# One-hots of four tokens from one VectorE comparison, with the gate's two parts multiplied in by GpSimd and ScalarE

## The chip, the cores and the metric

One NeuronCore of a Trainium2 chip runs the whole program. The metric is the device time of one launch in microseconds (us), less is better. In this text PE is TensorE (PEld its weight loads), DVE is VectorE, ACT is ScalarE, POOL is GpSimd, SP the engine that issues most DMAs.

## The reference

A two-layer encoder on 256 tokens of width 1024. Each layer has an attention part and then PEER, a retrieval of experts, and the change is in PEER alone. For each token, 8 heads choose 16 of 16384 experts each; an expert is a pair (i1, i2) of key numbers under 128:

```python
best, pos = lax.top_k(cand, PEER_TOPK)
expert = jnp.take_along_axis(cand_idx, pos, axis=-1)      # i1 * 128 + i2
gate = jax.nn.softmax(best, axis=-1)
...
u = w_down[e_blk]
a = jnp.einsum('td,ted->te', x_blk, u).astype(jnp.float32)
hg = (jax.nn.gelu(a, approximate=False) * g_blk).astype(w_up.dtype)
return jnp.einsum('te,ted->td', hg, w_up[e_blk]).astype(x_blk.dtype)
```

The output is the float32 result of both layers.

## The kernel before, in words

The kernel gathers no expert. It computes every expert for every token and multiplies by a gate that is zero for those not chosen. `peer(li)` runs twice, once for each layer, in this order:

1. Queries and key scores.
2. The loop over `b0` (lines 1017 to 1039): 128 blocks of 128 experts, two a round. A block is 24 matmuls of 128x256 (`d`, in `proj`): weights and x are each split into a high and a low fp32r part, and three of the four products are summed. ScalarE then takes the GELU of a round's two blocks into `A`, a view of the arena [128, block, token].
3. The up projection (`rows`, tile `y`), 128 blocks again.

Beside the first 50 or so blocks of the loop the generator `choose` finds the 128 (head, k) pairs of every token, mostly on VectorE. It ends with the gates and indices transposed, a pair on each partition and a token in each column (tile `gT`), and the lines 973 to 984: `gt` is the gate times 2^14, `g16`/`gh` its half-precision part, `gr` the rest as a share of that part, `i1t` and `i2t` the two key numbers.

From then on each round also **places** gates. `prepare(g4)` (lines 989 to 998) makes, for a group of four tokens, three half-precision matrices per token, [128 pairs, 128 keys]: V, the one-hot of i2; U, the one-hot of i1 times the gate; L, U times `gr`. V is made on GpSimd, U on VectorE (one instruction, comparison and product), L on ScalarE. `place(g4, done)` (lines 1000 to 1012) multiplies them on TensorE: for each token V is the stationary operand, U and L are moved through it and summed in a tile `G`, whose element [i2, i1] is the token's gate for that expert. `G` is multiplied into the blocks of `A` that have had their GELU already (L1011, VectorE, reading G and A) and copied into the columns of `A` of the blocks to come (L1009, ScalarE), where the later GELU is multiplied in (L1029 on ScalarE, L1030 on VectorE).

The loop places two groups in a round and then prepares the next two. `VU` and `U` come from the pool `ohp`, which has two buffers of each, so a group's one-hots can be made only after TensorE has read those of the group two before it, and they have to be there when TensorE comes to the G matmuls one round later. The weight stream `ws` works three blocks ahead in four buffers: a cast to `hi` on ScalarE (L97), `lo` = raw - hi on VectorE (L101). The order of instructions on each engine is found by a scheduler at build time, except where a chain fixes it. Each engine then works its queue in that order.

Of the kernel before, what the change touches and what calls it, by code (L numbers as in the profile page):

```python
# [10 lines left out]
F32 = mybir.dt.float32  # L11
F32R = mybir.dt.float32r
F16 = mybir.dt.float16
U32 = mybir.dt.uint32
AF = mybir.ActivationFunctionType
ALU = mybir.AluOpType
AX = mybir.AxisListType

P = 128
T = 256  # L20
# [5 lines left out]
NKEYS = 128  # L26
# [18 lines left out]
WARM = 9  # L45
EARLY = 11264
GSCALE = 2.0 ** 14
TINY = 2.0 ** -40
DSA_POOL = 3
MAGIC = 12582912.0  # L50

# [111 lines left out]
def tile_trunk(ctx: ExitStack, tc: tile.TileContext, ins, out: bass.AP):  # L163
    nc = tc.nc
    def pool(name, bufs, **kw):
        return ctx.enter_context(tc.tile_pool(name=name, bufs=bufs, **kw))

    const = pool("const", 1)
# [3 lines left out]
    ohp = pool("ohp", 2)  # L172
# [9 lines left out]
    def ps(name):  # L182
        return psp.tile([P, 512], F32, tag="ps", name=name)

    def py(i, name):
        return pyp.tile([P, 512], F32, tag=f"py{i}", name=name)
# [5 lines left out]
    keep = [dram.tile([P, D], F32, tag=f"x{t}", name=f"x{t}") for t in range(2)]  # L192
    xh = const.tile([P, NC, T], F32R, tag="xh", name="xh")
    xl = const.tile([P, NC, T], F32R, tag="xl", name="xl")
    i1t = const.tile([P, T], F32, tag="i1t", name="i1t")
    i2t = const.tile([P, T], F32, tag="i2t", name="i2t")
    gt = const.tile([P, T], F32, tag="gt", name="gt")
    gr = const.tile([P, T], F32, tag="gr", name="gr")
    iota16 = const.tile([P, P], F16, tag="iota16", name="iota16")
    iotac = const.tile([P, CELLS, TOPK], F16, tag="iotac", name="iotac")  # L200
    arena = big.tile([P, 32768], F32, tag="arena", name="arena")
# [39 lines left out]
    def pe(emit):  # L241
        return link("pe", emit)
# [4 lines left out]
    def mm(o, l, r, start, stop):  # L247
        return pe(lambda: nc.tensor.matmul(o, l, r, start=start, stop=stop, skip_group_check=True))  # L248
# [606 lines left out]
    def peer(li):  # L855
# [14 lines left out]
        hot = ar.ring(2, TOPK, CELLS)  # L870
# [4 lines left out]
        tail = s[0].rearrange("p a b -> p (a b)")  # L875
# [46 lines left out]
        def choose():  # L922
            for t in range(2):
# [21 lines left out]
                for h in range(HEADS + 1):  # L945
                    if h < HEADS:
                        o, same = hot(), eq[h % 2]
                        nc.vector.tensor_tensor(same, iotac, pos16[t][:, h, None, :].to_broadcast([P, CELLS, TOPK]),  # L948
                                                op=ALU.is_equal)
# [20 lines left out]
                nc.tensor.transpose(pg[:, tsl], best[t].rearrange("p h k -> p (h k)"), ident)  # L970
                nc.tensor.transpose(pg[:, T + t * P : T + (t + 1) * P], exp_[t].rearrange("p h k -> p (h k)"), ident)
            e = pg[:, T:]
            g16, gh, gl = tail[:, 0 : T // 2].bitcast(F16), tail[:, T : 2 * T], tail[:, 2 * T : 3 * T]
            nc.vector.tensor_scalar(gt, pg[:, :T], GSCALE, None, op0=ALU.mult)
            nc.vector.tensor_copy(g16, gt)
            nc.vector.tensor_copy(gh, g16)
            nc.vector.tensor_tensor(gl, gt, gh, op=ALU.subtract)
            nc.vector.tensor_scalar(gh, gh, TINY, None, op0=ALU.max)
            nc.vector.reciprocal(gr, gh)
            nc.vector.tensor_tensor(gr, gr, gl, op=ALU.mult)  # L980
            nc.vector.tensor_scalar(i1t, e, 1.0 / NKEYS, -(NKEYS - 1) / (2.0 * NKEYS), op0=ALU.mult, op1=ALU.add)
            nc.vector.tensor_scalar(i1t, i1t, MAGIC, None, op0=ALU.add)
            nc.vector.tensor_scalar(i1t, i1t, -MAGIC, None, op0=ALU.add)
            nc.vector.scalar_tensor_tensor(i2t, i1t, -float(NKEYS), e, op0=ALU.mult, op1=ALU.add)  # L984
            yield

        onehot = {}

        def prepare(g4):
            hot16 = ohp.tile([P, 2, 4, P], F16, tag="V", name="VU")  # L990
            low16 = ohp.tile([P, 4, P], F16, tag="U", name="U")
            onehot[g4] = []
            for t in range(4 * g4, 4 * g4 + 4):
                V, U, L = hot16[:, 0, t % 4, :], hot16[:, 1, t % 4, :], low16[:, t % 4, :]
                nc.gpsimd.tensor_scalar(V, iota16, i2t[:, t : t + 1], None, op0=ALU.is_equal)  # L995
                nc.vector.tensor_scalar(U, iota16, i1t[:, t : t + 1], gt[:, t : t + 1], op0=ALU.is_equal, op1=ALU.mult)  # L996
                nc.scalar.mul(L, U, gr[:, t : t + 1])  # L997
                onehot[g4].append((V, U, L))

        def place(g4, done):  # L1000

            p = py(g4 % 4, f"G{g4}")
            for j, (V, U, L) in enumerate(onehot.pop(g4)):
                mm(p[:, j * P : (j + 1) * P], V, U, True, False)
                mm(p[:, j * P : (j + 1) * P], V, L, False, True)
            pv = p.rearrange("p (t b) -> p b t", b=P)
            tsl = slice(4 * g4, 4 * g4 + 4)
            if done < P:
                nc.scalar.mul(A[:, done:, tsl], pv[:, done:, :], 1.0 / GSCALE)  # L1009
            if done:  # L1010
                nc.vector.scalar_tensor_tensor(A[:, :done, tsl], pv[:, :done, :], 1.0 / GSCALE, A[:, :done, tsl],  # L1011
                                               op0=ALU.mult, op1=ALU.mult)

        bg = choose()
        groups = prepared = 0
        ready = False
        for b0 in range(0, NKEYS, 2):
            p = ps(f"d{b0}")
            pv = p.rearrange("p (j t) -> p j t", t=T)
            for j in range(2):  # L1020
                proj(pv[:, j, :], ws.get())
                for _ in range(STEPS[(b0 + j) % len(STEPS)]):
                    if not ready and next(bg, StopIteration) is StopIteration:
                        ready = True
            t0 = 4 * groups
            if t0 < T:
                nc.scalar.activation(A[:, b0 : b0 + 2, t0:], pv[:, :, t0:], AF.Gelu)
            if t0 > 0:
                nc.scalar.activation(pv[:, :, :t0], pv[:, :, :t0], AF.Gelu)  # L1029
                nc.vector.tensor_tensor(A[:, b0 : b0 + 2, :t0], A[:, b0 : b0 + 2, :t0], pv[:, :, :t0], op=ALU.mult)  # L1030
            while groups < prepared:
                place(groups, b0 + 2)
                groups += 1
            if ready:
                left = max(1, (NKEYS - 8 - b0) // 2)
                want = min(64 - groups, -(-(64 - groups) // left))
                for _ in range(want):
                    prepare(prepared)
                    prepared += 1
# [170 lines left out]
```

## Time and profile before

| what | value |
|---|---|
| median of 3 runs | 1865.2 us (1864.09 to 1866.58) |
| the profiled execution's own time | 1863.45 us |
| its span, first to last instruction | 1861.6 us |
| granted TensorE clock, mean | 0.998 of full speed |
| busy: PE / DVE / ACT / POOL | 1838.8 / 1326.6 / 1050.9 / 565.4 us |
| first G matmul of layer 0, of layer 1 | at 312.9 us, at 1259.2 us |
| last G matmul | at 1478.4 us |

Busy time is the sum over the span of time in which an engine had an instruction of the program at work. A matmul's record is longer than the step from one to the next, since they are pipelined: a d matmul's record lasts 0.28 us, and 48 of them take 5.71 us. So TensorE's pace is read from the starts. Waits are named by what ended them.

### The profile page before, as it was taken

Reading aid. Unit: us, or ns where it says so; the run is one execution under the profiler, and the core shown is the slowest. Engines: PE = TensorE matmul, PEld = TensorE weight load, DVE = VectorE, ACT = ScalarE, POOL = GpSimd, SP = SyncE. Lnnn points to the kernel's source line nnn. Section 1 sums busy time; section 2 is a strip of 40 time slices with the busy share of each in tenths; the row PEclk is TensorE's granted clock in tenths of the full one; section 3 lists DMA queues with packets and bytes.
Section 4 is the critical chain, followed back from the end, with each engine's and each line's share of the span. In section 5 each row is a group of like instructions: output and inputs, shape, how many; then the busy total and the mean of one; then the engine's idle time right before and its main releaser. Section 6 shows DMA issues by size and latency. Waiting matters only on the chain. (4 is left out here: it accounts for less than half of the span.)

```text
span 1861.6 us, 33296 instructions
## 1 busy us (share of the span) xinstructions
PE 1838.8 (99%) x12495; PEld 1653.3 (89%) x12495; DVE 1326.6 (71%) x2738; ACT 1050.9 (56%) x1826; POOL 565.4 (30%) x646
## 2 busy tenths in 40 slices
PE   9999999999999999999999999999999999999998
PEld 8899999999998888888888899999999988888886
DVE  6689986788865555555687789957888765555555
ACT  6655456777764444444466445548777654444443
POOL 2002443999930000000021004519999600000000
PEclk9999999999999999999999999999999999999999
DMA  6554655444456555556646455554444575555553
GB/s 236 192 175 166 192 194 180 150 154 154 158 194 213 189 186 191 186 187 191 205 154 227 153 169 181 175 196 153 159 151 157 169 229 190 186 189 191 184 190 114
DMA packets 93474, 335.52 MB, mean 180 GB/s; under 512 B 10368, under 2 KB 11392, under 8 KB 93312
## 3 DMA queue, kind: packets, MB, share of 16 engines
q1 hardware_dynamic: 93024, 332.87, 54.4%
q8 instruction: 98, 1.61, 0.4%
q14 instruction: 64, 0.52, 0.1%
q10 hardware_dynamic: 288, 0.52, 0.1%
HBM read 329.16 MB, written 4.19 MB: 179 GB/s over the span
## 5 line engine op out<-in xcount | busy, mean ns | idle before, releaser
L101 DVE TENSOR_TENSOR lo<-raw,hi 128x1024 fp32r<-128x1024 f32 (+1 forms) x581 | 715.7, 1234 | 341.9 <-ACT hi L97 341.2
L97 ACT CAST hi<-raw 128x1024 fp32r<-128x1024 f32 (+1 forms) x583 | 609.8, 1047 | 580.1 <-PE d L248 255.3
L248 PE MATMUL d<-xh,hi 128*128 128x256 f32 x2048 | 579.4, 283 | 0.0
L248 PE MATMUL d<-xh,lo 128*128 128x256 f32 x2048 | 573.0, 280 | 0.6 <-DVE lo L101 0.6
L248 PE MATMUL d<-xl,hi 128*128 128x256 f32 x2048 | 573.3, 280 | 0.0
L995 POOL TENSOR_SCALAR VU<-iota,i2t 128x128 f16<-128x128 f16 x512 | 430.0, 858 | 110.8 <-DVE i2t L984 98.8
L248 PEld LDWEIGHTS d<-xh,lo 128*128 128x128 f32 x2048 | 384.7, 188 | 1.0 <-DVE lo L101 1.0
L248 PEld LDWEIGHTS d<-xh,hi 128*128 128x128 f32 x2048 | 385.1, 188 | 0.0
L248 PEld LDWEIGHTS d<-xl,hi 128*128 128x128 f32 x2048 | 384.6, 188 | 0.0
L248 PE MATMUL y<-hi,xh 128*128 128x512 f32 x1088 | 344.3, 395 | 0.1
L248 PE MATMUL y<-lo,xh 128*128 128x512 f32 x1088 | 344.2, 395 | 0.0
L248 PE MATMUL y<-hi,xl 128*128 128x512 f32 x1088 | 343.8, 394 | 0.0
L339 POOL TENSOR_TENSOR st<-st,mhalf 128x1 f32<-128x1 f32 x8 | 4.4, 554 | 853.3 <-DVE st L337 853.3
L248 PEld LDWEIGHTS y<-lo,xh 128*128 128x128 f32 x1088 | 203.7, 187 | 50.1 <-DVE lo L101 0.3
L248 PEld LDWEIGHTS y<-hi,xl 128*128 128x128 f32 x1088 | 203.7, 187 | 50.0
L248 PEld LDWEIGHTS y<-hi,xh 128*128 128x128 f32 x1088 | 203.3, 187 | 50.1 <-DVE xl L276 0.5
L996 DVE TENSOR_SCALAR VU<-iota,i1t,gt 128x128 f16<-128x128 f16 x512 | 139.5, 350 | 57.8 <-PE G L248 31.5
L997 ACT ACTIVATE U<-VU,gr 128x128 f16<-128x128 f16 x512 | 170.1, 399 | 0.8 <-DVE gr L980 0.7
L1051 ACT CAST xh<-arena 128x512 fp32r<-128x512 f32 x128 | 79.4, 621 | 154.5 <-PE y L248 149.2
L1052 DVE TENSOR_TENSOR xl<-arena,xh 128x512 fp32r<-128x512 f32 x128 | 88.3, 693 | 82.2 <-ACT xh L1051 82.2
L950 POOL TENSOR_TENSOR arena<-arena 128x800 f32<-128x800 f16 x32 | 78.9, 2486 | 40.8 <-DVE arena L948 39.9
L248 PE MATMUL G<-VU 128*128 128x128 f16 x512 | 71.5, 222 | 6.3 <-DVE VU L996 3.7
(225 smaller groups left out, 1805.3 us busy)
## 6 DMA issues: line engine op xcount, KB each, us to landing
raw<-in_down SPq DMA_DIRECT2D x256, 512.0 KB, 3.3
raw<-in_up SPq DMA_DIRECT2D x256, 512.0 KB, 4.3
raw<-in_peer_q SPq DMA_DIRECT2D x24, 512.0 KB, 4.1
raw<-in_dsa_qk SPq DMA_DIRECT2D x16, 512.0 KB, 3.3
raw<-in_mla_w_o SPq DMA_DIRECT2D x8, 512.0 KB, 7.3
arena<-in_peer_q SPq DMA_DIRECT2D x8, 512.0 KB, 4.2
raw<-in_dsa_v SPq DMA_DIRECT2D x8, 512.0 KB, 4.4
raw<-in_dsa_w_o SPq DMA_DIRECT2D x8, 512.0 KB, 3.9
```

Of the source, the lines that this page charges most:

```text
L97: nc.scalar.copy(hi, raw)
L101: self.dve(lambda: nc.vector.tensor_tensor(lo, raw, hi.bitcast(F32), op=ALU.subtract))
L248: return pe(lambda: nc.tensor.matmul(o, l, r, start=start, stop=stop, skip_group_check=True))
L339: nc.gpsimd.tensor_tensor(st[:, 5:6], st[:, 4:5], mhalf, op=ALU.pow)
L950: nc.gpsimd.tensor_tensor(o.rearrange("p k c -> p c k"), same, cell[t][:, h, :, None].to_broadcast([P, CELLS, TOPK]), op=ALU.mult)
L995: nc.gpsimd.tensor_scalar(V, iota16, i2t[:, t : t + 1], None, op0=ALU.is_equal)
L996: nc.vector.tensor_scalar(U, iota16, i1t[:, t : t + 1], gt[:, t : t + 1], op0=ALU.is_equal, op1=ALU.mult)
L997: nc.scalar.mul(L, U, gr[:, t : t + 1])
L1051: nc.scalar.copy(hh, a)
L1052: nc.vector.tensor_tensor(al, a, hh.bitcast(F32), op=ALU.subtract)
```

## The change

- `prepare` makes both one-hots of four tokens, of i2 and of i1, with one VectorE comparison of 128x1024 elements (tile `hot`). Both its inputs and its output are 16-bit: `iota16` is repeated over the eight one-hots, and each token's index over 128 elements. The indices are kept as half-precision numbers in `place16`.
- The gate no longer enters in the comparison. GpSimd multiplies the four one-hots of i1 by the half-precision gates (one product of 128x512, tile `gate`, part 0). ScalarE multiplies the same one-hots by the rest, `rest` = gt - gate16, token by token (part 1).
- `place` makes the same matmuls: `hot[:, 0]` stationary, the two parts of `gate` moved.
- The lines after the transposes get shorter: no clamp, no reciprocal, no product with it.

```diff
@@ -45,7 +45,6 @@
 WARM = 9
 EARLY = 11264
 GSCALE = 2.0 ** 14
-TINY = 2.0 ** -40
 DSA_POOL = 3
 MAGIC = 12582912.0
 
@@ -192,10 +191,9 @@
     keep = [dram.tile([P, D], F32, tag=f"x{t}", name=f"x{t}") for t in range(2)]
     xh = const.tile([P, NC, T], F32R, tag="xh", name="xh")
     xl = const.tile([P, NC, T], F32R, tag="xl", name="xl")
-    i1t = const.tile([P, T], F32, tag="i1t", name="i1t")
-    i2t = const.tile([P, T], F32, tag="i2t", name="i2t")
-    gt = const.tile([P, T], F32, tag="gt", name="gt")
-    gr = const.tile([P, T], F32, tag="gr", name="gr")
+    place16 = const.tile([P, 2, T], F16, tag="place16", name="place16")
+    gate16 = const.tile([P, T], F16, tag="gate16", name="gate16")
+    rest = const.tile([P, T], F32, tag="rest", name="rest")
     iota16 = const.tile([P, P], F16, tag="iota16", name="iota16")
     iotac = const.tile([P, CELLS, TOPK], F16, tag="iotac", name="iotac")
     arena = big.tile([P, 32768], F32, tag="arena", name="arena")
@@ -970,39 +968,38 @@
                 nc.tensor.transpose(pg[:, tsl], best[t].rearrange("p h k -> p (h k)"), ident)
                 nc.tensor.transpose(pg[:, T + t * P : T + (t + 1) * P], exp_[t].rearrange("p h k -> p (h k)"), ident)
             e = pg[:, T:]
-            g16, gh, gl = tail[:, 0 : T // 2].bitcast(F16), tail[:, T : 2 * T], tail[:, 2 * T : 3 * T]
+            gt, i1 = tail[:, 0:T], tail[:, T : 2 * T]
             nc.vector.tensor_scalar(gt, pg[:, :T], GSCALE, None, op0=ALU.mult)
-            nc.vector.tensor_copy(g16, gt)
-            nc.vector.tensor_copy(gh, g16)
-            nc.vector.tensor_tensor(gl, gt, gh, op=ALU.subtract)
-            nc.vector.tensor_scalar(gh, gh, TINY, None, op0=ALU.max)
-            nc.vector.reciprocal(gr, gh)
-            nc.vector.tensor_tensor(gr, gr, gl, op=ALU.mult)
-            nc.vector.tensor_scalar(i1t, e, 1.0 / NKEYS, -(NKEYS - 1) / (2.0 * NKEYS), op0=ALU.mult, op1=ALU.add)
-            nc.vector.tensor_scalar(i1t, i1t, MAGIC, None, op0=ALU.add)
-            nc.vector.tensor_scalar(i1t, i1t, -MAGIC, None, op0=ALU.add)
-            nc.vector.scalar_tensor_tensor(i2t, i1t, -float(NKEYS), e, op0=ALU.mult, op1=ALU.add)
+            nc.vector.tensor_copy(gate16, gt)
+            nc.vector.tensor_tensor(rest, gt, gate16, op=ALU.subtract)
+            nc.vector.tensor_scalar(i1, e, 1.0 / NKEYS, -(NKEYS - 1) / (2.0 * NKEYS), op0=ALU.mult, op1=ALU.add)
+            nc.vector.tensor_scalar(i1, i1, MAGIC, None, op0=ALU.add)
+            nc.vector.tensor_scalar(i1, i1, -MAGIC, None, op0=ALU.add)
+            nc.vector.tensor_copy(place16[:, 1, :], i1)
+            nc.vector.scalar_tensor_tensor(place16[:, 0, :], i1, -float(NKEYS), e, op0=ALU.mult, op1=ALU.add)
             yield
 
         onehot = {}
 
         def prepare(g4):
-            hot16 = ohp.tile([P, 2, 4, P], F16, tag="V", name="VU")
-            low16 = ohp.tile([P, 4, P], F16, tag="U", name="U")
-            onehot[g4] = []
-            for t in range(4 * g4, 4 * g4 + 4):
-                V, U, L = hot16[:, 0, t % 4, :], hot16[:, 1, t % 4, :], low16[:, t % 4, :]
-                nc.gpsimd.tensor_scalar(V, iota16, i2t[:, t : t + 1], None, op0=ALU.is_equal)
-                nc.vector.tensor_scalar(U, iota16, i1t[:, t : t + 1], gt[:, t : t + 1], op0=ALU.is_equal, op1=ALU.mult)
-                nc.scalar.mul(L, U, gr[:, t : t + 1])
-                onehot[g4].append((V, U, L))
+            hot = ohp.tile([P, 2, 4, P], F16, tag="V", name="hot")
+            gate = ohp.tile([P, 2, 4, P], F16, tag="U", name="gate")
+            four = slice(4 * g4, 4 * g4 + 4)
+            nc.vector.tensor_tensor(hot, iota16[:, None, None, :].to_broadcast([P, 2, 4, P]),
+                                    place16[:, :, four, None].to_broadcast([P, 2, 4, P]), op=ALU.is_equal)
+            nc.gpsimd.tensor_tensor(gate[:, 0], hot[:, 1], gate16[:, four, None].to_broadcast([P, 4, P]), op=ALU.mult)
+            for j in range(4):
+                t = 4 * g4 + j
+                nc.scalar.mul(gate[:, 1, j, :], hot[:, 1, j, :], rest[:, t : t + 1])
+            onehot[g4] = hot, gate
 
         def place(g4, done):
 
             p = py(g4 % 4, f"G{g4}")
-            for j, (V, U, L) in enumerate(onehot.pop(g4)):
-                mm(p[:, j * P : (j + 1) * P], V, U, True, False)
-                mm(p[:, j * P : (j + 1) * P], V, L, False, True)
+            hot, gate = onehot.pop(g4)
+            for j in range(4):
+                for i in range(2):
+                    mm(p[:, j * P : (j + 1) * P], hot[:, 0, j, :], gate[:, i, j, :], i == 0, i == 1)
             pv = p.rearrange("p (t b) -> p b t", b=P)
             tsl = slice(4 * g4, 4 * g4 + 4)
             if done < P:
```

The build also puts instructions in another order. Line numbers of the changed kernel are one to three lower for the same statement.

VectorE, a placing round in the middle of layer 0, before. VU are the one-hots, lo the low weight parts, L1011 and L1030 the products with G and with d:

```order
L996 TENSOR_SCALAR VU<-iota_96,i1t,gt 128x128 x8
L101 TENSOR_TENSOR lo_6590<-raw_6395,hi_6589 128x1024
L1011 SCALAR_TENSOR_TENSOR arena<-G_6538,arena 128x106x4
L1011 SCALAR_TENSOR_TENSOR arena<-G_6549,arena 128x106x4
L1030 TENSOR_TENSOR arena<-arena,d_6474 128x2x192
L101 TENSOR_TENSOR lo_6620<-raw_6479,hi_6619 128x1024
L996 TENSOR_SCALAR VU<-iota_96,i1t,gt 128x128 x8
```

And now, in a placing round of the same layer:

```order
L988 TENSOR_TENSOR hot<-iota_95,place_92 128x1024 x2
L100 TENSOR_TENSOR lo_4846<-raw_4675,hi_4845 128x1024
L1008 SCALAR_TENSOR_TENSOR arena<-G_4806,arena 128x78x4
L1008 SCALAR_TENSOR_TENSOR arena<-G_4817,arena 128x78x4
L1027 TENSOR_TENSOR arena<-arena,d_4742 128x2x80
L100 TENSOR_TENSOR lo_4876<-raw_4747,hi_4875 128x1024
L988 TENSOR_TENSOR hot<-iota_95,place_92 128x1024 x2
```

Two comparisons of 1024 elements stand where eight of 128 stood; the rest of the round keeps its order.

TensorE, the first placing round of layer 0, before. G_3802 and G_3813 are the first two groups, d_3852 the block pair of that round:

```order
L248 LDWEIGHTS VU
L248 MATMUL G_3802<-U,VU 128x128
L248 LDWEIGHTS VU
L248 MATMUL G_3802<-VU 128x128
L248 MATMUL d_3852<-xh,hi_3681 128x256
L248 LDWEIGHTS VU
L248 MATMUL G_3802<-U,VU 128x128
L248 LDWEIGHTS VU
L248 MATMUL G_3802<-VU 128x128
L248 MATMUL d_3852<-xl,hi_3681 128x256
```

And now, the end of the same two groups and the d matmuls behind them:

```order
L246 LDWEIGHTS hot
L246 MATMUL G_3797<-gate,hot 128x128
L246 LDWEIGHTS hot
L246 MATMUL G_3797<-gate,hot 128x128
L246 MATMUL d_3824<-xh,hi_3677 128x256
L246 MATMUL d_3824<-xl,hi_3677 128x256
L246 MATMUL d_3824<-xh,lo_3678 128x256
L246 MATMUL d_3824<-xh,hi_3677 128x256
```

Before, the G matmuls of the first two rounds were scattered among those of d; now each round has its 16 in one piece, from the first on. From the third round on both kernels read 16 of G, 48 of d.

## Rows read from the trace of the kernel before

**Rows 1.** The page, part 1: busy us (share of the span) xinstructions.

```profile
PE 1838.8 (99%) x12495; PEld 1653.3 (89%) x12495; DVE 1326.6 (71%) x2738; ACT 1050.9 (56%) x1826; POOL 565.4 (30%) x646
```

**Rows 2.** The chain that ended last, in order of time: start, us, what.

```profile
1466.35 5.71 PE d L248 x48
1472.07 0.46 PE G L248 x8
```

**Rows 3.** Timeline of PE, first G matmuls of rounds: start, us, engine, line, operation.

```profile
312.91 0.23 PE L248 MATMUL G<-VU 128*128 128x128 f16 x1
...
335.38 0.23 PE L248 MATMUL G<-VU 128*128 128x128 f16 x1
342.00 0.23 PE L248 MATMUL G<-VU 128*128 128x128 f16 x1
...
525.19 0.23 PE L248 MATMUL G<-VU 128*128 128x128 f16 x1
1259.22 0.23 PE L248 MATMUL G<-VU 128*128 128x128 f16 x1
...
1281.70 0.23 PE L248 MATMUL G<-VU 128*128 128x128 f16 x1
...
1471.91 0.23 PE L248 MATMUL G<-VU 128*128 128x128 f16 x1
```

**Rows 4.** Waits: who waited for whom; us in total, times, longest.

```profile
PEld L248 <- POOL VU L995: 12.0, 33, 0.7
```

**Rows 5.** Groups by line, 335.38 to 525.19 us: count, busy us, mean ns, idle before.

```profile
L995 POOL TENSOR_SCALAR VU<-iota,i2t 128x128 f16<-128x128 f16 x225 | 189.4, 859 | 2.4 <-PE G L248 2.0
L997 ACT ACTIVATE U<-VU,gr 128x128 f16<-128x128 f16 x224 | 74.7, 399 | 0.0
```

**Rows 6.** Timelines of PE, DVE and POOL in one placing round.

```profile
403.18 0.23 PE L248 MATMUL G<-VU 128*128 128x128 f16 x1
403.89 2.06 DVE L996 TENSOR_SCALAR VU<-iota,i1t,gt 128x128 f16<-128x128 f16 x8 [0.69 <-PE G L248]
404.88 0.66 POOL L995 TENSOR_SCALAR VU<-iota,i2t 128x128 f16<-128x128 f16 x1
405.88 1.21 DVE L101 TENSOR_TENSOR lo<-raw,hi 128x1024 fp32r<-128x1024 f32 x1
406.12 1.44 POOL L995 TENSOR_SCALAR VU<-iota,i2t 128x128 f16<-128x128 f16 x1
407.01 0.91 DVE L1011 SCALAR_TENSOR_TENSOR arena<-G,arena 128x336 f32<-128x336 f32 x2
```

**Rows 7.** Timelines of POOL and DVE, in choose of layer 0 and in dsa.

```profile
255.03 1.72 POOL L950 TENSOR_TENSOR arena<-arena 128x800 f32<-128x800 f16 x1 [0.43 <-DVE arena L948]
255.71 1.98 DVE L101 TENSOR_TENSOR lo<-raw,hi 128x1024 fp32r<-128x1024 f32 x1
...
930.84 0.69 DVE L495 TENSOR_TENSOR arena<-qi,arena 128x512 f32<-128x512 f32 x1 [1.16 <-ACT arena L492]
930.89 1.30 POOL L496 TENSOR_TENSOR arena<-arena 128x512 f32<-128x512 f32 x1 [19.88 <-ACT arena L492]
```

**Rows 8.** Timelines of DVE and POOL, in dsa, 982.8 to 985.

```profile
982.86 1.21 DVE L101 TENSOR_TENSOR lo<-raw,hi 128x1024 fp32r<-128x1024 f32 x1
983.78 1.45 POOL L496 TENSOR_TENSOR arena<-arena 128x512 f32<-128x512 f32 x1 [3.84 <-ACT arena L492]
984.00 1.38 DVE L801 TENSOR_SCALAR arena<-arena 128x256 f32<-128x256 f32 x1
```

**Rows 9.** Two lines: count, ns min/median/max, first and last start, forms.

```profile
L948 DVE TENSOR_TENSOR arena<-iotac,arena x32: 552/590/1070, 179.4 to 1198.4; 128x800 f16<-128x800 f16 x32
L496 POOL TENSOR_TENSOR arena<-arena x13: 742/1297/1908, 28.2 to 1003.8; 128x512 f32<-128x512 f32 x12, 128x256 f32<-128x256 f32 x1
```

**Rows 10.** Two lines of the placing rounds, same columns.

```profile
L1011 DVE SCALAR_TENSOR_TENSOR arena<-G,arena x128: 386/513/659, 318.3 to 1480.4; 128x232 f32<-128x232 f32 x4, 128x240 f32<-128x240 f32 x4, 128x248 f32<-128x248 f32 x4, 128x256 f32<-128x256 f32 x4
L1030 DVE TENSOR_TENSOR arena<-arena,d x70: 157/438/684, 325.4 to 1498.0; 128x512 f32<-128x512 f32 x6, 128x16 f32<-128x16 f32 x2, 128x32 f32<-128x32 f32 x2, 128x48 f32<-128x48 f32 x2
```

## The prediction

> **What bounds the kernel now.** I read the page's head first: TensorE is busy for 1838.8 us, 99% of the span, so time can only be won where TensorE waits or runs in a worse order [rows 1]. The chain of waits then tells what a stretch without loss looks like: 48 products of d take 5.71 us, eight of G 0.46 us [rows 2]. The change touches only the placing stretch of the two peer layers, in which every round of two blocks runs 16 G products and 48 d products. I went through TensorE's timeline for the starts of G groups [rows 3]. A good round takes 342.00 - 335.38 = 6.62 us. The 28 rounds from 335.38 to 525.19 take 189.81 us where 28 x 6.62 = 185.36 would do: 4.45 us lost; in layer 1, 1281.70 to 1471.91 is 190.21: 4.85 us lost. Ahead of them stand three rounds' worth of products (144 of d, 48 of G) in 335.38 - 312.91 = 22.47 and 1281.70 - 1259.22 = 22.48 us, against 3 x 6.62 = 19.86: 2.61 and 2.62 us lost. Together **14.5 us** of the whole run.
>
> Who causes it: TensorE's weight loads wait on GpSimd's one-hots [rows 4], and GpSimd has almost no idle time in the 189.81 us: its 225 comparisons keep it busy for 189.4 us, 0.859 each, while ScalarE's 224 products take 74.7 us [rows 5]. Eight comparisons by 0.859 are 6.87 us a round, more than TensorE's 6.62. So GpSimd sets the round, not TensorE. A comparison alone takes 0.66 us; one that meets VectorE's subtraction lo of 405.88 takes 1.44 [rows 6]: GpSimd stands still while that runs.
>
> **The port.** This sharing decides what the new code costs. While a GpSimd product of two SBUF inputs runs from 255.03 to 256.75, lo of 255.71 takes 1.98 us, not 1.22: it starts at 256.47, 0.28 before GpSimd ends [rows 7]. A VectorE operation with one input in PSUM is untouched: L495 takes its 0.69 us beside a GpSimd product of 1.30 [rows 7]. So two-input work from SBUF runs on one of the two engines at a time. Who goes first: the GpSimd product of 983.78 finds lo at work until 984.07 and takes 1.45 us, 0.15 over its 1.30; VectorE's next operation, issued at 984.00, then takes 1.38 and so lets GpSimd through [rows 8]. The engine that waited goes first.
>
> **Part by part.**
> - *GpSimd*: 512 comparisons go, 128 products of 128x512 come. Bounds for one: 512/800 of the 1.72 us row, 1.10 [rows 7]; the median of 128x512 f32 products, 1.30 [rows 9]. I take 1.20, midway. Two a round are 2.4 us in place of 6.87.
> - *VectorE*: eight comparisons a round (2.06 us together [rows 6]) go, two of 1024 elements come. Bounds for one: L948 compares 800 16-bit pairs in 0.552 us when alone [rows 9], which is 0.7 us for 1024; lo has 1024 elements and takes 1.22 [rows 6]. I take 1.22: in the new operation one index stands still for 128 elements, which makes it unlike L948, whose two inputs both run on. [...]
> - *ScalarE*: still eight products a round, 74.7 / 224 = 0.33 us each [rows 5]. They now stand in one block ahead of a hi, not around it. The first four can start when the first comparison ends (1.92, below), the others when the second does (3.06), so the last ends at 4.4 to 4.7, two microseconds ahead of the next G. The hi behind them and its lo feed a block three ahead, so TensorE does not wait for it.
> - *TensorE*: same products, in groups of 16 from the first round. This and an unhindered GpSimd would return all 14.5 us.
> - *Index chain*: four operations less and one more, on 256 elements. The first G follows the transposes by 96 products of d, twice 5.71 us [rows 2], which cover it before and now; nothing lies on the path. DMAs and SP's queue are unchanged.
>
> **What is late next.** VectorE's order in a round is: comparison, comparison, lo, two products with G (L1011), one with d (L1030), lo. The first comparison starts 0.7 us after the first G product, when that buffer is read (403.18 and 403.89, [rows 6]); operations follow 0.08 us before the end of the one before, so those of 1.22 come every 1.14 us. The second comparison ends at 3.06. The first gate product, waiting, starts 0.14 before that, at 2.92, and lo waits until 0.28 before its end: 0.86 us of wait. The round of VectorE is thus 4 x 1.14 + 0.86 + S = 5.42 + S, with S the other three. S grows over the 31 rounds: L1011 from 0.386 to about 0.62 (0.659 at the very last), L1030 from 0.157 to about 0.65 [rows 10]; less 0.08 each, S goes from 0.70 to 1.65, by 0.031 a round. VectorE's round passes 6.62 when S passes 1.20, in the last 14.5 rounds: 0.45 x 14.5 / 2 = 3.3 us behind by the end. lo then runs from 3.84 to 5.06, the second gate product from 4.92 to 6.12, while the second group is wanted at 6.62 + 0.44 = 7.06, so the first 0.9 us are free. **2.4 us** a layer remain as stalls, 4.8 in all. With 1.30 a product it is 4.1 a layer, with 1.10 it is 1.0.
>
> **Sum.** 14.5 - 4.8 = 9.7 us less. The profiled execution took 1863.45 us, so 1853.7 against it; it lies 1.75 us under the median of the runs shown, 1865.2, against which I forecast **1855.5 us**. The two bounds of a gate product give 1858.9 and 1852.7.
>
> **Rivals.**
> - *A, the comparison runs at L948's pace* (0.7). Each round of VectorE is 1.04 us shorter, at most 6.0, and nothing waits: all 14.5 us, **1850.7 us**. For it: L948 has 16-bit operands and a broadcast input too. Against: the index that stands still. [...]
> - *B, VectorE keeps the port* (slower). lo follows the second comparison without a break, and the row of 984.00 is one case only. If lo goes first (2.98 to 4.20), both gate products run behind it from 4.06 on, and the second lo starts 0.28 before their end: VectorE's round is 1.14 + 1.14 + 1.22 - 0.14 + 2g - 0.28 + 1.14 = 4.22 + 2g for a gate product of g. At 1.20 it just holds; at 1.30 it costs 0.2 us in 31 rounds and is still faster; from 1.33 it is slower. At 1.40 (over the f32 rows, as GpSimd's f16 operation is slow, see C) 0.4 x 31 - 0.6 = 11.8 a layer, 23.6 - 14.5 = 9.1 us more: **1874.3 us**.
> - *C, a gate product is slower than the f32 rows* (same). It reads and writes f16, and its gate stands still as well; GpSimd's f16 operation here costs 0.66 us for only 128 elements. At 1.45 the wait is 1.11, VectorE is behind from S = 0.95 in 22.6 rounds, 0.70 x 22.6 / 2 = 7.9, less 0.7: 7.2 a layer, which eats the gain: **1865 us**.
>
> That the edit does not do what it says is no rival: the order printed shows the comparisons off GpSimd's queue.
>
> **How the numbers follow.** Forecast 0.48, A 0.22, C 0.15, B 0.15. A measurement of this kernel can tell about 0.2%, 3.7 us, from no change. The forecast with its bounds and A are faster by more than that (0.66, a little off for a forecast that ends short), C and that little are within it (0.18), B and a heavier C are slower (0.16). The range goes from A less 1 us, about the scatter of the runs, into B, leaving out its upper half: 1849.5 to 1872.
>
> **What would show it.** Right: rounds of 6.62 us from the first G group on, GpSimd idle for more than half of the stretch, comparisons of about 1.22 us, the first lo of a round near 2.1 us as it waits for a gate product, and short TensorE waits on GpSimd only in the last third of the placing rounds. Comparisons near 0.7 us show A; a gate product that starts only after lo shows B; gate products over 1.4 us beyond their waits show C. Wrong altogether would be d products at another pitch than 5.7 us for 48, or TensorE waiting for ScalarE's products.

## The result and the profile after

The changed kernel takes **1851.83 us** (median of 4 runs, 1850.26 to 1852.3) against 1864.92 us before: a ratio of 0.9933, with a 95% interval of 0.9922 to 0.9945. The forecast was 1855.5 us, the range 1849.5 to 1872. The profiled execution took 1852.3 us over a span of 1850.4, 11.15 us less than the 1863.45 of before.

Part 1 of the page [rows 1]: VectorE has 58 us more to do, GpSimd's records add up to 178 us less, and TensorE is busy for 7 us less while it does the same matmuls.

```profile
PE 1831.6 (99%) x12495; PEld 1652.0 (89%) x12495; DVE 1384.4 (75%) x2348; ACT 1051.7 (57%) x1826; POOL 387.4 (21%) x262
```

The timeline of PE, first G matmul of rounds of layer 0 [rows 3]:

```profile
314.55 0.23 PE L246 MATMUL G<-gate,hot 128*128 128x128 f16 x1
321.16 0.23 PE L246 MATMUL G<-gate,hot 128*128 128x128 f16 x1
...
493.28 0.23 PE L246 MATMUL G<-gate,hot 128*128 128x128 f16 x1
500.13 0.23 PE L246 MATMUL G<-gate,hot 128*128 128x128 f16 x1
507.07 0.23 PE L246 MATMUL G<-gate,hot 128*128 128x128 f16 x1
513.82 0.23 PE L246 MATMUL G<-gate,hot 128*128 128x128 f16 x1
521.03 0.28 PE L246 MATMUL G<-gate,hot 128*128 128x128 f16 x2
```

Rounds last 6.62 us from the first one on, and only the last four are longer: 6.85, 6.94, 6.75 and 7.21. The 31 rounds from 314.55 to 521.03 take 206.48 us, in layer 1 (1253.97 to 1460.45) again 206.48. Before, the same stretch took 212.28 and 212.69 us [rows 3]. At 6.62 a round it would be 205.22. Below, the **loss** of a kernel is what this stretch takes beyond 205.22: 7.06 + 7.47 = 14.5 us before, 1.26 + 1.26 = 2.5 us after. That is 12.0 us less, while the two profiled executions differ by 11.15; what took 0.9 back is, as far as it is known, in the last section.

The groups by line from 314.55 to 521.03 us [rows 5], and a round in the middle on VectorE and GpSimd [rows 6]:

```profile
L990 POOL TENSOR_TENSOR gate<-hot,gate 128x512 f16<-128x512 f16 x62 | 122.1, 1987 | 86.0 <-DVE hot L988 86.0
L988 DVE TENSOR_TENSOR hot<-iota,place 128x1024 f16<-128x1024 f16 x62 | 73.0, 1218 | 3.0 <-PE G L246 2.6
```

```profile
401.33 2.36 DVE L988 TENSOR_TENSOR hot<-iota,place 128x1024 f16<-128x1024 f16 x2
402.64 3.94 POOL L990 TENSOR_TENSOR gate<-hot,gate 128x512 f16<-128x512 f16 x2 [2.68 <-DVE hot L988]
403.61 2.06 DVE L100 TENSOR_TENSOR lo<-raw,hi 128x1024 fp32r<-128x1024 f32 x1
405.60 0.91 DVE L1008 SCALAR_TENSOR_TENSOR arena<-G,arena 128x336 f32<-128x336 f32 x2
406.43 0.35 DVE L1027 TENSOR_TENSOR arena<-arena,d 128x208 f32<-128x208 f32 x1
406.71 1.21 DVE L100 TENSOR_TENSOR lo<-raw,hi 128x1024 fp32r<-128x1024 f32 x1
407.95 2.36 DVE L988 TENSOR_TENSOR hot<-iota,place 128x1024 f16<-128x1024 f16 x2
```

A comparison takes 1.22 us. GpSimd's two products are recorded as 3.94 us, but each stands still for almost half of its time (1.97 us against 1.03 for the shortest such product in e4, below): the first is issued at 402.64 and, by that 1.03, begins about when the second comparison ends (401.33 + 2.36 = 403.69), the second about when lo ends (405.67). lo in turn takes 2.06 us in place of 1.21, as it waits for the first product. VectorE's list, from one pair of comparisons to the next, is 6.5 us of work, just inside the 6.62 of the round, and the products with G and with d (L1008, L1027) grow from round to round. Late in the layer, on the same engines:

```profile
509.59 2.35 DVE L988 TENSOR_TENSOR hot<-iota,place 128x1024 f16<-128x1024 f16 x2
510.88 3.94 POOL L990 TENSOR_TENSOR gate<-hot,gate 128x512 f16<-128x512 f16 x2 [3.06 <-DVE hot L988]
511.86 2.06 DVE L100 TENSOR_TENSOR lo<-raw,hi 128x1024 fp32r<-128x1024 f32 x1
513.84 1.18 DVE L1008 SCALAR_TENSOR_TENSOR arena<-G,arena 128x464 f32<-128x464 f32 x2
514.94 0.62 DVE L1027 TENSOR_TENSOR arena<-arena,d 128x464 f32<-128x464 f32 x1
515.48 1.21 DVE L100 TENSOR_TENSOR lo<-raw,hi 128x1024 fp32r<-128x1024 f32 x1
516.62 2.35 DVE L988 TENSOR_TENSOR hot<-iota,place 128x1024 f16<-128x1024 f16 x2
```

There VectorE works without a break and needs 516.62 - 509.59 = 7.03 us. The waits that are left [rows 4], and the chain of work that ended last around one of them [rows 2], show the same from TensorE's side: the waits for the one-hots are for the gate product, and they lie in these rounds. The first line counts only 1.3 us of them; the second has the whole 2.5, as idle time of the weight loads, in eight gaps (four a layer, each at the start of a round's second group) for which the profile names no releaser.

```profile
PE G L246 <- POOL gate L990: 1.3, 6, 0.4
PEld L246 <- issue: 2.5, 8, 0.5
```

```profile
508.48 2.33 PE d L246 x21
510.81 0.07 issue
510.88 3.95 POOL gate L990 x2
514.83 0.04 issue
514.87 0.61 PE G L246 x8
```

The chain goes from TensorE to GpSimd and does not name VectorE. That GpSimd had waited 3.06 us for VectorE's comparison before the product of 510.88 stands in that product's own row above.

### The profile page after: what moved, and what is told of

Its sections match the earlier page's. It is cut to its first block, busy times and chain, and to the rows that moved or that the text cites. A ratio compares the mean times of both kernels' runs of the same rounds, so it can differ in the third digit from the quotient of the medians.

```text
span 1850.4 us, 32339 instructions
## 1 busy us (share of the span) xinstructions
PE 1831.6 (99%) x12495; PEld 1652.0 (89%) x12495; DVE 1384.4 (75%) x2348; ACT 1051.7 (57%) x1826; POOL 387.4 (21%) x262
## 4 chain that ended last, share of the span: by engine, by line
PE 94%; DVE 2%; POOL 2%; issue 1%; ACT 1%; DMA 0%; SPq 0%; DVEq 0%; POOLq 0%; ACTq 0%
PE y L246 41%; PE d L246 37%; PE pq L246 4%; PE G L246 3%; PE q L246 2%; POOL gate L990 2%; PE v L246 1%; PE qw L246 1%; PE ps L246 1%; PE s L246 1%; PE h L246 1%; PE qi L246 1%; DVE lo L100 1%; PE qn L246 0%; PE o L246 0%
## 5 line engine op out<-in xcount | busy, mean ns | idle before, releaser
L100 DVE TENSOR_TENSOR lo<-raw,hi 128x1024 fp32r<-128x1024 f32 (+1 forms) x581 | 768.7, 1325 | 324.8 <-ACT hi L96 324.5
L990 POOL TENSOR_TENSOR gate<-hot,gate 128x512 f16<-128x512 f16 x128 | 251.9, 1986 | 278.0 <-DVE hot L988 278.0
L993 ACT ACTIVATE gate<-hot,rest 128x128 f16<-128x128 f16 x512 | 156.8, 394 | 25.3 <-DVE hot L988 25.0
L988 DVE TENSOR_TENSOR hot<-iota,place 128x1024 f16<-128x1024 f16 x128 | 152.6, 1231 | 6.5 <-PE G L246 5.8
L246 PE MATMUL G<-gate,hot 128*128 128x128 f16 x1024 | 69.9, 220 | 1.5 <-POOL gate L990 1.3
```

What stands on the lines that cost most here:

```text
L100: self.dve(lambda: nc.vector.tensor_tensor(lo, raw, hi.bitcast(F32), op=ALU.subtract))
L988: nc.vector.tensor_tensor(hot, iota16[:, None, None, :].to_broadcast([P, 2, 4, P]), place16[:, :, four, None].to_broadcast([P, 2, 4, P]), ...
L990: nc.gpsimd.tensor_tensor(gate[:, 0], hot[:, 1], gate16[:, four, None].to_broadcast([P, 4, P]), op=ALU.mult)
L993: nc.scalar.mul(gate[:, 1, j, :], hot[:, 1, j, :], rest[:, t : t + 1])
```

## The experiments

The theory after the result: before, GpSimd's V one-hots set the pace of the stretch, lengthened by VectorE's instructions with two SBUF inputs; taking them away returns the loss, and what is left comes from VectorE late in the stretch. Its rivals: the gain came from the tidier order of TensorE in the first rounds; or GpSimd's records only look long, and neither engine holds the other up. The results in one table (loss as defined above, from the profiled execution of each; where a kernel ran in several rounds its median, otherwise one run):

| kernel | loss, layer 0 | layer 1 | time, us |
|---|---|---|---|
| before | 7.06 | 7.47 | 1864.2 to 1865.1 |
| changed | 1.26 | 1.26 | 1851.83 |
| e1, before with the order alone | 5.62 | 5.96 | 1861.61 |
| e2, before with V on VectorE | 11.41 | 12.09 | 1871.88 |
| e3, changed with paired indices | 0.00 | 0.00 | 1849.24 |
| e4, gate product twice | 47.65 | 49.45 | 1946.11 |
| e5, gate product token by token | 96.96 | 96.69 | 2043.63 |
| e6, gate product on VectorE | 9.72 | 9.71 | 1868.86 |
| e7, changed with the comparison split | 23.73 | 23.73 | 1895.56 |

The chain that fixes TensorE's order, shown under e1, is also in e2, e4, e5 and e6. The diffs below show only the lines that matter. Left out besides the chain: e2 keeps `i2t` in half precision, e5 makes one float32 copy of the gates, and e3 writes each index twice.

The time follows the loss: e7's 47.5 us are 33 more than the 14.5 of before, and it takes 30.5 us more.

### e1: the order alone

In the kernel before, TensorE's instructions are chained in program order from the first placing round on, so that 16 G matmuls follow each other:

```diff
+                chains.setdefault("pe", None)
                 place(groups, b0 + 2)
...
+        chains.pop("pe")
```

> The kernel before, with one thing changed: TensorE takes the sixteen G matmuls of a round in one run from the first round on, as it does in the changed kernel, and the one-hots are made as before. The theory (GpSimd's V one-hots bound the placing stretch from its first round, 256 of them at 0.859 us, so the opening's scattered order of matmuls cost nothing by itself): no gain over 1 us, 1863.5 to 1865.5 us, TensorE still waiting for V in every round. The rival (the opening's 2.6 us a layer came from the scattered order): 5.2 us less, about 1859.5 us.

Measured: 1861.61 us against 1864.56 (ratio 0.9987, 0.9977 to 0.9996). Both expectations missed: the order is worth 1.44 + 1.51 = 2.95 us, not under 1 and not 5.2. The timeline of POOL, before and then in e1, shows how an order on TensorE reaches GpSimd:

```profile
305.34 7.77 POOL L995 TENSOR_SCALAR VU<-iota,i2t 128x128 f16<-128x128 f16 x8 [48.59 <-DVE i2t L984]
316.15 2.67 POOL L995 TENSOR_SCALAR VU<-iota,i2t 128x128 f16<-128x128 f16 x3 [3.04 <-issue]
```

```profile
305.28 7.79 POOL L995 TENSOR_SCALAR VU<-iota,i2t 128x128 f16<-128x128 f16 x8 [48.58 <-DVE i2t L984]
313.62 5.93 POOL L995 TENSOR_SCALAR VU<-iota,i2t 128x128 f16<-128x128 f16 x8 [0.56 <-POOL VU L995]
...
320.46 13.06 POOL L995 TENSOR_SCALAR VU<-iota,i2t 128x128 f16<-128x128 f16 x15 [0.91 <-PE G L248]
```

With its first groups scattered among d matmuls, TensorE reads the first buffers late, and GpSimd stands idle for 3.04 us with nothing to write into; in the tidy order it stands for 0.56 + 0.91 = 1.47 us. The difference, 1.57, is the 1.44 us that layer 0 gains. So the order pays because it lets the slowest engine start sooner. In the later rounds GpSimd still holds TensorE up, about every second time: 11.6 of the 14.5 us stay.

```profile
PEld L248 <- POOL VU L995: 9.7, 30, 0.4
```

### e2: V on VectorE

The kernel before with the same order, and V of four tokens by one comparison of VectorE. GpSimd does nothing in the stretch.

```diff
+            nc.vector.tensor_tensor(hot16[:, 0], iota16[:, None, :].to_broadcast([P, 4, P]),
+                                    i2t[:, four, None].to_broadcast([P, 4, P]), op=ALU.is_equal)
...
-                nc.gpsimd.tensor_scalar(V, iota16, i2t[:, t : t + 1], None, op0=ALU.is_equal)
```

> The kernel before, in the tidy order of the run above, with V of four tokens made by one 128x512 comparison on VectorE, so that GpSimd has nothing to do in the stretch. The theory: no wait for GpSimd is left and the first rounds come at 6.62 us. VectorE's round is then 2.06 (eight U) + 2 x 0.61 (V) + 2 x 1.14 (lo, with nobody else at the port) + S = 5.56 + S, S going from 0.70 to 1.65, so it falls behind in about the last 20 rounds, by 0.59 x 20 / 2 less 0.9 of slack = 5 us a layer: about 10 of the 14.5 us are lost again, late instead of early, and the time is about 1860 us (1856 to 1862). The rival that GpSimd did not bound: rounds of more than 6.62 us from the start, and 1864 us or more.

Measured: 1871.88 us (ratio 1.0049, 1.0034 to 1.0064), slower than before, where 1860 was expected. The middle came as expected: from 324.11 us on twenty rounds in a row last 6.62 us, where before and in e1 such rounds alternate with longer ones. So GpSimd was what held those. The start of the first and the end of the last, 20 x 6.62 = 132.4 us apart:

```profile
324.11 0.23 PE L248 MATMUL G<-VU 128*128 128x128 f16 x1
...
456.51 0.23 PE L248 MATMUL G<-VU 128*128 128x128 f16 x1
```

Both ends were mis-sized. The first round takes 9.77 us, in layer 1 10.67, as TensorE waits for ScalarE's L (it lies in the tile named U), which waits for `gr`, and that now stands behind more work in VectorE's queue (its last step starts at 315.13 us; before, at 311.00):

```profile
316.30 0.22 PE L248 MATMUL G<-U,VU 128*128 128x128 f16 x1 [1.73 <-ACT U L999]
```

The last ten rounds lose 8 us a layer where 5 were expected. Here, too, TensorE waits for ScalarE's L (16 such waits in the run, 12.7 us), which come after VectorE's U. Without the gate taken out of the comparison, V on VectorE is no gain.

### e3 and e7: the rate of the comparison

What is left after the change should be VectorE's. e3 stores every index twice side by side, and compares in two instructions a group, the gates' index first, so that the innermost step reads two neighbouring elements. e7 makes the same split without the pairs.

```diff
-    place16 = const.tile([P, 2, T], F16, tag="place16", name="place16")
+    place16 = const.tile([P, 2, T, 2], F16, tag="place16", name="place16")
...
+            for i in (1, 0):
+                nc.vector.tensor_tensor(
+                    hot[:, i].rearrange("p t (b c) -> p t b c", c=2),
+                    iota16.rearrange("p (b c) -> p b c", c=2)[:, None].to_broadcast([P, 4, P // 2, 2]),
+                    place16[:, i, four, None, :].to_broadcast([P, 4, P // 2, 2]), op=ALU.is_equal)
```

> The changed kernel with every index stored twice side by side, and a group's comparison made as two 128x512 instructions (the one for the gates' index first) whose innermost step reads two neighbouring elements in place of one that is repeated. The theory: it then runs at two results a cycle, 0.35 to 0.45 us each, some 0.7 us a group in place of 1.22; VectorE's round falls to 4.5 + S, never above 6.2, so the 2.8 us that TensorE still waits late in both layers go: 1849 us, 2 to 3 less than the changed kernel. The rival (the repeated element was not what held the rate): 0.69 us each and 1852 to 1855 us.

Measured: 1849.24 us, ratio to before 0.9923 (0.9909 to 0.9936). The loss is gone in both layers. But the reason expected for it is half wrong. The line of the comparison (count, ns min/median/max), and a round on VectorE and GpSimd:

```profile
L990 DVE TENSOR_TENSOR hot<-iota,place x256: 408/419/1269, 307.3 to 1455.2; 128x512 f16<-128x512 f16 x128
```

```profile
400.91 2.28 DVE L990 TENSOR_TENSOR hot<-iota,place 128x512 f16<-128x512 f16 x4
401.42 1.16 POOL L994 TENSOR_TENSOR gate<-hot,gate 128x512 f16<-128x512 f16 x1 [3.94 <-DVE hot L990]
402.93 1.16 POOL L994 TENSOR_TENSOR gate<-hot,gate 128x512 f16<-128x512 f16 x1 [0.36 <-DVE hot L990]
403.11 2.06 DVE L100 TENSOR_TENSOR lo<-raw,hi 128x1024 fp32r<-128x1024 f32 x1
...
508.29 2.26 DVE L990 TENSOR_TENSOR hot<-iota,place 128x512 f16<-128x512 f16 x4
515.23 2.27 DVE L990 TENSOR_TENSOR hot<-iota,place 128x512 f16<-128x512 f16 x4
```

A comparison takes 0.42 us for 512 elements in place of 1.22 for 1024. With the element repeated, e7 takes 0.68 for 512. The traces give times and no results a cycle, so that part of the expectation is not shown; its 0.35 to 0.45 us is. Yet the four comparisons together still take 2.28 us, against 2.36 for the two of the changed kernel: the third now waits for the first gate product and lasts up to 1.27 us. VectorE's round hardly gets shorter (late in the layer 515.23 - 508.29 = 6.94 us against 7.03, still more than TensorE's 6.62). What moved is GpSimd: its second product ends 402.93 + 1.16 - 400.91 = 3.18 us after the first comparison starts, in the changed kernel 402.64 + 3.94 - 401.33 = 5.25. The 2 us between them are slack in which VectorE's lateness disappears.

> The changed kernel with a group's comparison made as two 128x512 instructions, the one for the gates' index first, as in the run with the paired indices, but with the indices stored once, so that each compares against a repeated element. In that earlier run VectorE's round was hardly shorter than in the changed kernel, since a comparison now waited for GpSimd too (four of them 2.28 us, then lo 2.06). The question is whether the gain there came from the rate or from the split. If from the rate: each comparison lasts 0.69 (0.61 to the next), the second pair waits 0.83 for the first gate product and lo 0.83 for the second, VectorE's round is 4 x 0.61 + 0.83 + 0.83 + 2 x 1.14 + S = 6.4 + S, above 6.62 from the first round, and some 25 us a layer are lost: 1890 to 1910 us. If the split alone brings the gate products forward far enough: 1848 to 1852 us.

Measured: 1895.56 us (ratio 1.017, 1.0153 to 1.0187), as expected from the rate. The line of the comparison, and VectorE in one round:

```profile
L989 DVE TENSOR_TENSOR hot<-iota,place x256: 675/680/1531, 305.6 to 1503.0; 128x512 f16<-128x512 f16 x128
```

```profile
400.70 3.33 DVE L989 TENSOR_TENSOR hot<-iota,place 128x512 f16<-128x512 f16 x4
403.95 2.06 DVE L100 TENSOR_TENSOR lo<-raw,hi 128x1024 fp32r<-128x1024 f32 x1
```

The split puts two waits of some 0.85 us for GpSimd into VectorE's round (one among the comparisons, one in lo). At 0.68 a comparison the four take 3.33 us, and TensorE's rounds pass 6.62 from the seventh on; at 0.42 the same two waits fit. So e3's gain needs the rate, which makes the split affordable; the split then brings the gate products forward. The rate without the split was not tried.

The two kernels were then run beside each other on one chip, in five rounds each:

> The changed kernel once more, as the measure for the next run on one chip. 1850 to 1853 us, some 1.25 us of TensorE's waits between the first and the last G of each layer.

> The kernel with the indices stored in pairs once more, beside the changed kernel on one chip. The theory: its stretch from the first G to the last takes 211.4 us in both layers where the changed kernel takes 212.65, so it is 2.5 us faster, 0.13%. The rival (the shorter stretch is given back elsewhere): no difference.

Measured: 1852.62 us (1848.55 to 1854.02) and 1849.55 us (1846.84 to 1852.51), against 1864.19 before; ratios 0.9942 (0.9928 to 0.9956) and 0.9924 (0.991 to 0.9938). The loss is 1.27 and 1.06 in the one, nothing in the other, as expected. The paired version came out faster here by 3.1 us, about the size of the loss that it removes; the intervals of the times overlap, so the traces carry this, not the times alone. It has the lowest medians of this study.

### e4: GpSimd's product twice

```diff
-            nc.gpsimd.tensor_tensor(gate[:, 0], hot[:, 1], gate16[:, four, None].to_broadcast([P, 4, P]), op=ALU.mult)
+            for _ in range(2):
+                nc.gpsimd.tensor_tensor(gate[:, 0], hot[:, 1], gate16[:, four, None].to_broadcast([P, 4, P]), op=ALU.mult)
```

> The changed kernel with each of GpSimd's gate products done twice over, in the same place, and the same order of TensorE. The theory (GpSimd and VectorE's two-SBUF-input instructions keep each other out: a product of 1.05 us that meets one lasts 1.9 to 2.0): a round's four products last about 1.97 + 1.97 + 1.05 + 1.97 = 7.0 us behind a first comparison of 1.3, the second group's one-hots come 7 to 8.5 us into a round of 6.62, and 0.4 to 1.9 us is lost in each of 62 rounds: 1875 to 1960 us. The rival (the products only looked long while they waited for the comparison, and run beside VectorE's work): four products of 1.05 end 5.7 us into the round, no new wait, 1851 to 1854 us.

Measured: 1946.11 us, in one run. The line of the product, and one round of GpSimd:

```profile
L991 POOL TENSOR_TENSOR gate<-hot,gate x256: 1034/1902/2117, 308.1 to 1554.3; 128x512 f16<-128x512 f16 x128
```

```profile
473.35 6.92 POOL L991 TENSOR_TENSOR gate<-hot,gate 128x512 f16<-128x512 f16 x4 [1.16 <-DVE hot L988]
```

Undisturbed a product takes 1.03 us; four of those would have had room in the round. They take 6.92, as 7.0 was expected, and from the twelfth round on nearly every round of TensorE is 8.08 us. So the waits are real, not an effect of how the first product is recorded.

### e5: the gate product token by token

```diff
-            nc.gpsimd.tensor_tensor(gate[:, 0], hot[:, 1], gate16[:, four, None].to_broadcast([P, 4, P]), op=ALU.mult)
+            for j in range(4):
+                t = 4 * g4 + j
+                nc.gpsimd.tensor_scalar(gate[:, 0, j, :], hot[:, 1, j, :], gate32[:, t : t + 1], None, op0=ALU.mult)
```

> The changed kernel, in a fixed order of TensorE, with GpSimd's gate product made token by token with a scalar operand: eight instructions a round that read one SBUF input each, as the V one-hots of the kernel before did. The theory (GpSimd needs the same port for those, and each VectorE instruction with two SBUF inputs holds one of them up for its whole 1.05 to 1.15 us): eight of about 0.6 and four encounters (two comparisons, two lo) are 4.8 + 4.4 = 9.2 us of GpSimd a round, more than before the change (two encounters, 6.9), so some 2.0 to 3.4 us are lost in each of 62 rounds: 1975 to 2060 us. The rival (0.86 us is what such an instruction costs in itself): 6.9 us a round, about 0.3 lost in each, some 1870 us.

Measured: 2043.63 us, in one run. GpSimd's instructions, then VectorE's comparisons and its lo, the last in the stretch of layer 0 (ns min/median/max):

```profile
L994 POOL TENSOR_SCALAR gate<-hot,gate x512: 592/598/2609, 310.2 to 1649.2; 128x128 f16<-128x128 f16 x171
```

```profile
L990 DVE TENSOR_TENSOR hot<-iota,place x128: 1215/1226/1241, 308.8 to 1644.6; 128x1024 f16<-128x1024 f16 x128
L100 DVE TENSOR_TENSOR lo<-raw,hi x65: 1215/1220/1361, 311.1 to 618.3; 128x1024 fp32r<-128x1024 f32 x65
```

GpSimd's instructions take 0.6 us in half of the cases, but up to 2.6 where two of VectorE's instructions follow each other, and the mean is 0.97: 7.7 us a round, not the 9.2 expected. The rest of the loss was not expected: two rounds together take about 19.5 us, in which TensorE waits for the products (103.8 us in 148 waits over the run), GpSimd for its comparisons (32 waits) and the comparisons for buffers that GpSimd still holds (88.1 us in 56 waits), and from 330 to 620 us the mean granted clock was 0.85 (0.99 from 330 to 560 us in e4). How much of the loss the clock made was not separated. So the time lies in the expected range (1975 to 2060) partly by luck: less waiting of GpSimd for VectorE than expected, and losses that were not. The comparisons never exceed 1.24 us, and lo has a median of 1.22 and a longest of 1.36: here GpSimd's instructions with one SBUF input are held up by VectorE's with two (2.6 in place of 0.6), and hardly hold those up. In the changed kernel the product with two inputs does (lo 2.06).

### e6: the gate product on VectorE

```diff
-            nc.gpsimd.tensor_tensor(gate[:, 0], hot[:, 1], gate16[:, four, None].to_broadcast([P, 4, P]), op=ALU.mult)
+            nc.vector.tensor_tensor(gate[:, 0], hot[:, 1], gate16[:, four, None].to_broadcast([P, 4, P]), op=ALU.mult)
```

> The changed kernel, in a fixed order of TensorE, with the gate product on VectorE in place of GpSimd, which then has nothing to do. The theory: VectorE has no room for it late in the stretch. Its round is 4 x 1.14 + 2 x 0.61 + S = 5.8 + S, without waits at the port, past 6.62 from S = 0.82, in the last 27 of 31 rounds: 0.83 x 27 / 2 = 11 less some slack, 9 to 11 us a layer lost where the changed kernel loses 1.25, so 15 to 20 us slower than the changed kernel: 1867 to 1872 us, with the first ten rounds or more at 6.62. The rival (VectorE is busy for 75% only and has room): 1850 to 1853 us.

Measured: 1868.86 us (ratio 1.0027, 1.0017 to 1.0037), with a loss of 9.7 us a layer, as expected, and thirteen rounds at 6.62 us before it begins. TensorE's waits for weights, which before named GpSimd, now name VectorE:

```profile
PEld L246 <- DVE gate L990: 21.0, 26, 1.3
```

The product needs 2 x 0.61 us a round there and takes away 0.85 of waiting; VectorE, 75% busy over the whole span, has no room for the difference late in this stretch. So the part of the change that leaves a product on GpSimd is worth 8.5 us a layer.

## Why the prediction was right

The sign, the place and the mechanism held; the time came out 3.7 us under the forecast, inside the range. By its steps:

- **GpSimd sets the round** [rows 4, 5]. Right for most of it: with GpSimd out of the way (e2) rounds of 6.62 us follow each other, and with the order of TensorE alone (e1) 11.6 of the 14.5 us of loss stay. Too simple for the first rounds: 2.95 us of the loss came by way of TensorE's scattered order. The prediction put both in one line ("same products, in groups of 16 from the first round") and so lost nothing by it.
- **The comparison at 1.22.** Right, 1.218; rival A's 0.7 did not come. The argument for it, that one index stands still, fits these traces: 1.22 us for 1024 elements in the changed kernel and 0.68 for 512 in e7, where one is repeated 128 times, and 0.42 for 512 in e3, where the innermost step repeats none.
- **The port.** Right: the first lo of a round takes 2.06 us, a wait of 0.85, forecast 0.86, and GpSimd, having waited, goes first. So rival B fell. The evidence for it was thinner than it looked: the VectorE instruction of 984.00 [rows 8], a TENSOR_SCALAR, has one SBUF input, not two, so that row showed who goes first, but not between two instructions of two inputs. A port as such stands in no trace; the traces show records that get longer beside each other.
- **The gate product at 1.20.** Mis-sized: 1.03 us by e4's shortest, under the lower bound of 1.10. The wait of lo came out right all the same, and that was luck, as two errors cancelled: the product is 0.17 us shorter, but lo starts only 0.14 us before the product's end (405.67 - 1.21 = 404.46, against 402.64 + 1.96), not 0.28. But the second product ends 5.97 us into the round (from the first G, 400.61, to 402.64 + 3.94), not 6.12. Rival C's 1.45 fell with it.
- **VectorE's round, 5.42 + S.** Right: 2.28 + 1.99 + 1.11 + 1.14 in the round shown, with S = 1.11, which makes 5.41 + S; in the late one S is 1.64, the forecast 1.65.
- **The loss that stays, 2.4 us a layer.** This is the term that failed: 1.26. hot starts 0.73 us behind G up to round 17 (counted from 0), one and a half rounds longer than forecast, and 2.04 behind in round 26, whose one-hots are the first to come late. The slack is 1.1 us, not 0.9, by the second product's earlier end. And the sum ran to the last round, while the last two groups are placed one to a round (521.03 and 527.20), so that the last, latest pair delays nothing. The difference, 2.3 us in both layers, is most of the 3.7; the rest is no more than the scatter of single runs described below.
- **Signs.** Rounds, comparisons, lo and late waits came as named. "GpSimd idle for more than half of the stretch" was wrong by the record: 122.1 us of 206.5 are busy, though by e4's shortest only 62 x 1.03 = 64 of them are its own work. The sign forgot that GpSimd is recorded as busy while it waits for VectorE (a product's median is 1.96 us).

## What to carry to other kernels

An instruction's time in the profile may be mostly waiting for another engine (in e5 GpSimd's instructions took 0.6 us in half of the cases and up to 2.6 beside VectorE's): look at what runs beside the long records before moving work. The shortest record of a line is no more than an upper bound of its own cost, which shows only where nothing runs beside it: in the changed kernel every gate product waits, none is under 1.89 us, and it took e4 to see 1.03. Read whether an engine has room from the stretch and the round in which it is fullest, not from its share of the span: VectorE's 75% hid rounds of over 100%. Where a 16-bit comparison repeats one element, storing that element in pairs can raise its rate: here a comparison of 512 elements went from 0.68 us (e7) to 0.42 (e3).

## What was not expected

- The product of two SBUF inputs and the one of one input behave differently beside VectorE: GpSimd's two-input product and VectorE's two-input instructions hold each other up (lo 2.06, gate 1.96), while GpSimd's one-input instructions are held up and hardly hold those up (e5: up to 2.6 in place of 0.6, comparisons 1.24 at most). The two kinds also differ in operation and size, so that the number of inputs decides is not shown by itself.
- VectorE's own instructions with one SBUF input are not free of GpSimd either. The U comparison of the kernel before, beside GpSimd's V, and then in e2, where GpSimd did nothing in the stretch (ns min/median/max):

```profile
L996 DVE TENSOR_SCALAR VU<-iota,i1t,gt x512: 297/317/741, 305.1 to 1468.5; 128x128 f16<-128x128 f16 x171
L998 DVE TENSOR_SCALAR VU<-iota,i1t,gt x512: 302/309/318, 306.9 to 1475.8; 128x128 f16<-128x128 f16 x171
```

In e2 none is over 0.32 us; before, about a quarter take 0.43 us or more, up to 0.74, although GpSimd's V has one SBUF input too. In rows 8 a VectorE scalar operation of 256 elements took 1.38 us, to 0.15 us after the end of a GpSimd product (983.78 + 1.45 = 985.23). So which form of VectorE's instruction it is also matters; what decides it was not tried.
- The d matmuls have two paces at the same granted clock. The matmuls of d started between 262 and 298 us, ahead of anything that the change touches, in the changed kernel and then in its second profiled execution:

```profile
262.00:298.00 36.00, 36.00 (x308) 1.00 0.65 214
```

```profile
262.00:298.00 36.00, 36.00 (x320) 1.00 0.68 222
```

The same code makes 308 in one execution and 320 in the other, 117.8 and 113.3 ns apart, and the kernel before made 320. This is where the profiled execution of the changed kernel gave back some of its 12.0 us: its first G comes at 314.55 us, that of before at 312.91, that of the second execution at 312.90. What sets the pace was not tried; it moves single runs by about 2 us a layer and is no effect of the change.
